# A hybrid RWKV-7 and attention block in fp32 on one core: input norm reordered, POOL's two-tensor work taken out of attention, planner numbers changed

## The chip, the core and the metric

The kernel runs on one core of a Trainium2 chip. The metric is the device time of one execution in microseconds (us); of several executions the median counts. The profile is of one further execution. Its engines are PE (TensorE, matrix products), DVE (VectorE), ACT (ScalarE), POOL (GpSimd) and SP (SyncE, which here issues DMAs). "PEclk" is the clock that PE was granted, as a share of 2.4 GHz; it has two levels, 1.00 and 0.50 (1.2 GHz).

## The reference

```
h     = rms_norm(x, norm_g)                       # x: 512 tokens x 2048 channels
proj  = h @ w_in                                  # 11008 columns = 86 strips of 128
xr, xk, xv, wdown, adown = split(centred_shift(proj[..., :3328], mu))   # strips 0 to 25
z_r, q, k, v, z_a, gates = split(proj[..., 3328:])                      # strips 26 to 85
o_r   = rwkv7_bidir(xr, xk, xv, wdown, adown, ...) * silu(z_r)   # 16 heads of 64, scan over tokens both ways
o_a   = axial_gqa(q, k, v) * silu(z_a)                           # 16 query heads, 4 key heads of 64
merged = sigmoid(g_r) * (o_r @ w_branch_rwkv) + sigmoid(g_a) * (o_a @ w_branch_attn)
out   = rms_norm(x + merged @ w_out, final_norm_g)

def axial_gqa(q, k, v):            # in blocks of 128 queries
    q, k = rope(rms_norm(q)), rope(rms_norm(k))
    p = softmax(q k^T / 8)
    return p v
```

## The kernel before

**Products.** All large products are made in fp32 precision from three passes of a faster format (fp32r): each operand is split into a high part and the rest (`split`, L263: ACT casts the high part, L264; DVE, or POOL where `load` is told so, subtracts, L265). For each of 16 channel tiles of a strip PE does three matmuls of 128x512 (L291): high by high, low by high, high by low. A quarter of a strip is one DMA of 256 KB on SP's queue (`raw`), one cast `wh`, one subtraction `wl` and 12 matmuls. `hh` and `hl` are the high and low part of the normalised, transposed input.

**Stages.** (1) The norm: four tiles of 128 tokens (`x01`, `x23`) are loaded, squared and summed (ACT, partly DVE at L358), scaled by 1/rms in pieces of 512 columns (L371 on POOL, L373 on DVE), transposed by PE (`turn`, L383) and written as `hh` by ACT (L385) and `hl` by DVE (L386); two strips are multiplied beside it. While x is on its way, PE does `warm` transposes of a constant (L394). (2) The RWKV stage: 8 tiles of two heads each. For a tile `stage_a` squares the keys (`sq`, ACT L502), sums them per head on PE (`pss`, L507), takes the root on POOL and spreads it back over PE (`prb`, L516). `tile_task` builds the chunk matrices (`lr`, L637), transposes the factors `BK` to token-major (`tb`, L706), inverts small blocks on DVE (L680, L681) and walks 8 chunks: `pa` (L754), copy `a0s` on ACT, `pu` (L763), copies, `px2` (L770). `stage_e` normalises a tile's output, transposes it (`pg`, L816) and finishes it on DVE (`gc`, L819, L820). `sq` takes its buffer from a ring of four (`temp`) in which `gc` stands too. (3) Attention: 64 units of 128 queries of a head: scores `sc` (L961, L962), maximum on DVE (L964), exp on ACT (`pr`, L967), scaling on POOL (L970), transposes `pT` (L978), split `ph`, `pl` on ACT and DVE, product with the values `po` (L993). Beside it the 16 strips of the RWKV branch's projection are multiplied (`acc<-oq`, below R); their input `oq` takes the buffer of `hh` when the last input strip is done (`or_task`). The first strips of the attention branch's projection (`acc<-oah`, below A) start there as far as heads are done. (4) The rest of A with the merge (`tgm`, L1067, L1068), the output product (L1101 to L1103) and the final norm.

**Order.** PE's instructions stand in the order of the code up to the end of stage 2. A planner (`Weave`) sets that order with planned times: a task says after how many ns it wants to go on (`yield cost, wait, flag`), and in between PE gets "dense" matmuls of the strips (`Dense`), planned at 227 ns each. From stage 3 on a scheduler sets PE's order as well, as it does for the other engines everywhere, by planned times of its own. Each engine then works strictly in its order. `OPT` holds the numbers: `c1` is the planned wait between `pa` and `pu`, `warm` the count of warm-up transposes, `every=2` gives every second `wl` of the R strips and of the input strips left in stage 3 to POOL.

Of the kernel before, what the change touches and what calls it, by code (L numbers as in the profile page):

```python
# [213 lines left out]
OPT = dict(manual=True, tls=True, sub="dve", subwait=47000, fwait=6000, gn=22000, u1=0, u2=0, c1=700, c2=700, c3=1400, fly=3, scale='pool', prb=4, low=1300, warm=24, rwt='tile', every=2, auto=1, man=1)  # L214
# [10 lines left out]
def emit_all(nc, tc, A, out, dbg):  # L225
    ve, ac, po, pe, sp = nc.vector, nc.scalar, nc.gpsimd, nc.tensor, nc.sync

    def f(ap):
# [100 lines left out]
    with tc.tile_pool(name="xps", bufs=5, space=PSUM) as xps:  # L329
# [17 lines left out]
        po.memset(mhalf, -0.5)  # L347
        for tt in range(4):
            sq = rw.tile([128, D], F32, name="xsq", tag="bko")
            ss = rw.tile([128, 6], F32, name="ss", bufs=4)  # L350
            cut = {0: (D, D), 1: (1024, 1024), 2: (D, D), 3: (1024, 1536)}[tt]
            ac.activation(sq[:, 0:cut[0]], xt[tt][:, 0:cut[0]], AF.Square, accum_out=ss[:, 0:1])
            n = 1
            if cut[1] > cut[0]:
                ac.activation(sq[:, cut[0]:cut[1]], xt[tt][:, cut[0]:cut[1]], AF.Square, accum_out=ss[:, 1:2])
                n = 2
            if cut[1] < D:
                ve.scalar_tensor_tensor(out=sq[:, cut[1]:D], in0=xt[tt][:, cut[1]:D], scalar=1.0, in1=xt[tt][:, cut[1]:D],  # L358
                                        op0=ALU.mult, op1=ALU.mult, accum_out=ss[:, n:n + 1])
                n += 1  # L360
# [7 lines left out]
            for c in range(4):
                piece = xt[tt][:, c * 512:(c + 1) * 512]
                if tt == 2 or (tt == 3 and c == 3):  # L370
                    po.tensor_scalar(out=piece, in0=piece, scalar1=ss[:, 5:6], scalar2=0.0, op0=ALU.mult, op1=ALU.add)  # L371
                else:
                    ve.tensor_scalar(out=piece, in0=piece, scalar1=ss[:, 5:6], scalar2=None, op0=ALU.mult)  # L373
        ac.copy(blk, con[:, K_BLK:K_BLK + 128])
        ve.tensor_tensor(out=c0, in0=par[:, P_MU0:P_MU0 + 26], in1=par[:, P_MU1:P_MU1 + 26], op=ALU.add)
        ve.tensor_scalar(out=c0, in0=c0, scalar1=-1.0, scalar2=1.0, op0=ALU.mult, op1=ALU.add)
        ve.tensor_scalar(out=oka, in0=par[:, P_KA:P_KA + 8], scalar1=-1.0, scalar2=1.0, op0=ALU.mult, op1=ALU.add)
        ve.tensor_scalar(out=wah, in0=par[:, P_W0:P_W0 + 32], scalar1=0.5, scalar2=None, op0=ALU.mult)
# [110 lines left out]
    def stage_a(i):  # L489
# [121 lines left out]
    def tile_task(i):  # L611
# [90 lines left out]
        for d in range(2):  # L702
            for g in range(2):
# [334 lines left out]
    def share_r(d):  # L1038
# [132 lines left out]
```

## Time and profile before

| | |
|---|---|
| median of 3 runs | 1744.57 us (1742.69 to 1744.64) |
| the profiled execution | 1745.22 us |
| its span, first to last instruction | 1743.5 us |
| mean granted clock of PE | 0.99 |
| PE / DVE / ACT / POOL busy | 97% / 70% / 49% / 23% of the span |
| stage 1, norm | 0 to about 42 us |
| stage 2, RWKV tiles | to about 1190 us |
| stage 3, attention | to about 1473 us |
| stage 4, A strips, output product, final norm | to the end |

Everything that the span holds beyond PE's busy time is PE's waiting or the ends of the program. So the profile is read from PE's waits: how long, where in the stages, and what ended each. The second thing to read is the granted clock, since a matmul takes about twice as long at 0.50.

### The profile page before, as it was taken

How to read it: one execution, taken by the hardware profiler on the slowest of the kernel's cores; microseconds unless marked ns; L12 is line 12 of the kernel's file. 1: busy time of each engine (PE TensorE's matmuls, PEld its weight loads, DVE VectorE, ACT ScalarE, POOL GpSimd, SP SyncE). 2: the span in 40 equal slices, each digit the busy share in tenths (PEclk: the TensorE clock that was granted, in tenths of full speed). 3: DMA queues.
4: the chain of work that ended last, by engine and by line, in shares of the span. 5: the costliest groups of instructions: out<-in, count | busy, mean ns of one | idle time of the engine just before them, and what ended most of it. 6: DMA issues, size and time to landing. Idle time of an engine off the chain costs nothing. (4 is left out here: it accounts for less than half of the span.)

```text
span 1743.5 us, 26135 instructions
## 1 busy us (share of the span) xinstructions
PE 1694.3 (97%) x8972; PEld 1423.0 (82%) x8972; DVE 1212.0 (70%) x2437; ACT 849.1 (49%) x1955; POOL 393.4 (23%) x523
## 2 busy tenths in 40 slices
PE   7999999999999999999999999999999998999997
PEld 6888888888888887888887888888788887888876
DVE  6577779779689789689679679435888876443352
ACT  6555455455455454454454454544575655322241
POOL 2001031031131121121121121113555543331110
PEclk8999999999999999999999999999999998999999
DMA  6573323323323333333333324235343331444462
GB/s 218 167 230 105 108 60 116 104 80 104 101 85 104 92 91 91 91 98 100 94 93 93 94 67 121 86 103 169 97 133 108 99 97 61 136 130 134 127 181 103
DMA packets 96852, 194.89 MB, mean 112 GB/s; under 512 B 11088, under 2 KB 11344, under 8 KB 95312
## 3 DMA queue, kind: packets, MB, share of 16 engines
q1 hardware_dynamic: 77616, 152.18, 30.1%
q10 hardware_dynamic: 15264, 28.46, 4.5%
q0 software_dynamic: 3840, 12.59, 2.5%
q8 instruction: 72, 1.18, 0.3%
q14 instruction: 60, 0.49, 0.1%
HBM read 162.77 MB, written 30.41 MB: 111 GB/s over the span
## 5 line engine op out<-in xcount | busy, mean ns | idle before, releaser
L291 PE MATMUL acc<-hh,wl 128*128 128x512 f32 (+1 forms) x1388 | 551.6, 397 | 4.0 <-DVE wl L265 4.0
L291 PE MATMUL acc<-hl,wh 128*128 128x512 f32 (+1 forms) x1388 | 551.1, 397 | 2.4 <-DVE hl L386 2.1
L291 PE MATMUL acc<-hh,wh 128*128 128x512 f32 (+1 forms) x1388 | 552.5, 398 | 0.0
L264 ACT CAST wh<-raw 128x512 fp32r<-128x512 f32 x472 | 291.3, 619 | 428.4 <-PE acc L291 286.0
L265 DVE TENSOR_TENSOR wl<-raw,wh 128x512 fp32r<-128x512 f32 x442 | 316.4, 718 | 240.2 <-ACT wh L264 216.6
L291 PEld LDWEIGHTS acc<-hh,wl 128*128 128x128 f32 x1388 | 263.1, 190 | 55.0 <-DVE wl L265 6.1
L291 PEld LDWEIGHTS acc<-hl,wh 128*128 128x128 f32 x1388 | 263.1, 190 | 52.9 <-DVE hl L386 3.5
L291 PEld LDWEIGHTS acc<-hh,wh 128*128 128x128 f32 x1388 | 263.4, 190 | 49.6 <-ACT wh L264 0.3
L741 POOL TENSOR_SCALAR SV<-VT 64x128 f32<-64x128 f32 x256 | 137.4, 537 | 622.7 <-DVE SV L776 262.6
L776 DVE SCALAR_TENSOR_TENSOR SV<-SV,PC,px 64x64 f32<-64x64 f32 x224 | 62.7, 280 | 66.1 <-PE px L770 53.9
L681 DVE TENSOR_TENSOR B<-B,tm 128x30 f32<-128x30 f32 (+14 forms) x240 | 79.1, 330 | 5.4
L291 PE MATMUL acc<-oq,wh 128*128 128x512 f32 x256 | 82.7, 394 | 0.0
L680 DVE TENSOR_TENSOR tm<-B 128x30 f32<-128x30 f32 (+14 forms) x240 | 79.2, 330 | 5.0
L1102 PE MATMUL of<-wl,mh 128*128 128x512 f32 x192 | 74.9, 390 | 1.2 <-DVE wl L265 1.2
L1103 PE MATMUL of<-wh,ml 128*128 128x512 f32 x192 | 74.7, 389 | 0.0
L770 PEld LDWEIGHTS px<-SV,L 128*128 128x128 f32 x512 | 67.0, 191 | 6.9 <-ACT SV L764 1.5
L754 PEld LDWEIGHTS pa<-SV,AL 128*128 128x128 f32 x512 | 66.7, 191 | 4.8
L1101 PE MATMUL of<-wh,mh 128*128 128x512 f32 x192 | 66.1, 389 | 0.0
L754 PE MATMUL pa<-SV,AL 128*128 128x64 f32 x512 | 64.9, 269 | 0.0
L770 PE MATMUL px<-SV,L 128*128 128x64 f32 x512 | 64.7, 269 | 0.0
L291 PE MATMUL acc<-oah,wh 128*128 128x512 f32 x128 | 52.1, 409 | 5.5 <-ACT oah L264 3.4
L778 ACT COPY O<-px 64x128 f32<-64x128 f32 x64 | 16.7, 260 | 81.5 <-DVE SV L776 74.4
(686 smaller groups left out, 2744.1 us busy)
## 6 DMA issues: line engine op xcount, KB each, us to landing
raw<-in_w_in_dram SPq DMA_DIRECT2D x344, 256.0 KB, 3.2
raw<-in_wo_dram SPq DMA_DIRECT2D x64, 256.0 KB, 2.8
fsp<-tg ACTq DMA_DIRECT2D x60, 256.0 KB, 3.0
tsp<-la ACTq DMA_DIRECT2D x32, 256.0 KB, 3.8
la<-tsp SPq DMA_DIRECT2D x8, 1024.0 KB, 5.2
raw<-in_wbr_dram SPq DMA_DIRECT2D x32, 256.0 KB, 2.8
tgm<-fsp POOLq DMA_DIRECT2D x32, 256.0 KB, 3.5
raw<-in_wba_dram SPq DMA_DIRECT2D x32, 256.0 KB, 2.9
```

The lines of the kernel that those rows point to most:

```text
L264: ac.copy(dst_hi, src)
L265: (eng or ve).tensor_tensor(out=dst_lo, in0=src, in1=f(dst_hi), op=ALU.subtract)
L291: pe.matmul(acc[:, tok], lhsT=w[1 if u == 2 else 0][:, j, :], rhs=(xl if u == 1 else xh)[:, kt, tok], start=(kt == 0 and u == 0 and tok.st ...
L680: se.tensor_tensor(out=tv, in0=B[:, 0:s, s:s + 1].to_broadcast([128, s, n]), in1=B[:, s:s + 1, s + 1:32].to_broadcast([128, s, n]), op=ALU ...
L681: se.tensor_tensor(out=B[:, 0:s, s + 1:32], in0=B[:, 0:s, s + 1:32], in1=tv, op=ALU.add)
L741: mv = po.tensor_scalar(out=new[v0:v0 + 64, d, eo], in0=src.unsqueeze(1).to_broadcast([64, 2, C]), scalar1=1.0, scalar2=0.0, op0=ALU.mult, ...
L754: pe.matmul(pa[:, d, eo, :], lhsT=AL[:, d, cc[d], eo, :], rhs=SV[:, d, eo, 0, :], start=True, stop=True)
L770: pe.matmul(px2[:, d, eo, :], lhsT=L2[:, d, cc[d], eo, :], rhs=SV[:, d, eo, 1, :], start=True, stop=True)
L776: mn = ve.scalar_tensor_tensor(out=SN[h, d, eo, 0, :], in0=SV[h, d, eo, 0, :], scalar=PC[h, d, cc[d]:cc[d] + 1], in1=px2[h, d, eo, :], op0 ...
L1101: pe.matmul(acc, lhsT=mh[:, dt, tok(tt)], rhs=w[0], start=(dt == 0), stop=False)
L1102: pe.matmul(acc, lhsT=mh[:, dt, tok(tt)], rhs=w[1], start=False, stop=False)
L1103: pe.matmul(acc, lhsT=ml[:, dt, tok(tt)], rhs=w[0], start=False, stop=(dt == NKT - 1))
```

## The change

It touches five places.

- **Norm.** DVE's half of the squares of token tile 1 is written ahead of the scaling of tile 0; the scaling pieces of tiles 0 and 1 alternate by column (DVE); those of tiles 2 and 3 are written one by one at every fourth `turn` instead of ahead of all. The first `wl` goes to DVE instead of POOL. The small constants `c0`, `oka`, `wah` move behind the third `hl`. `warm` is 34 instead of 24.
- **RWKV tiles.** `c1` is 950 instead of 700. The wait ahead of `pss` is 7000 instead of 1500 (6000 for tile 0). The 16 `tb` transposes are visited twice by 8 instead of four times by 4.
- **Attention.** `every` is 0, so all `wl` are DVE's. `rotate` and the product of the heads' output with its gate move from POOL to DVE. The scaling of `pr` stays on POOL.
- **R strips.** Strips 14 and 15 may be planned only when unit 59 is through (flag `U59`).

```diff
-OPT = dict(..., c1=700, ..., warm=24, rwt='tile', every=2, auto=1, man=1)
+OPT = dict(..., c1=950, ..., warm=34, rwt='tile', every=0, auto=1, man=1)
...
-            first[i]["w"][q] = load(first[i], q, i == 0 and q == 0)
+            first[i]["w"][q] = load(first[i], q)
...
+        def normed(tt, c, by, eng):
+            piece = xt[tt][:, c * 512:(c + 1) * 512]
+            if eng is po:
+                po.tensor_scalar(out=piece, in0=piece, scalar1=by, scalar2=0.0, op0=ALU.mult, op1=ALU.add)
+            else:
+                ve.tensor_scalar(out=piece, in0=piece, scalar1=by, scalar2=None, op0=ALU.mult)
...
+            if tt == 1:
+                with tc.issue_after(half_.ins):
+                    for c in range(4):
+                        for t_ in range(2):
+                            normed(t_, c, inv_rms[t_], ve)
...
         for step in range(NKT):
-            turn(step, 0)
+            low_ = turn(step, 0)
             if 3 <= step < 15:
                 three(0, step - 3, slice(0, 256))
...
+            if step % 4 == 3:
+                normed(2, step // 4, inv_rms[2], po)
+                with tc.issue_after(low_.ins):
+                    normed(3, step // 4, inv_rms[3], ve if step < 12 else po)
...
-        yield 0, 1500 if i else 6000, None
+        yield 0, 7000, None
         pss = g_tile("pss")
...
                 ac.copy(L2b[:, d, 4 * g:4 * g + 4, 0:4:3, :], tb)
-                yield 428, 700, None
+                if g:
+                    yield 856, 1400, None
...
-        po.tensor_tensor(out=sw, in0=sw, in1=rope[:, 1], op=ALU.mult)
+        ve.tensor_tensor(out=sw, in0=sw, in1=rope[:, 1], op=ALU.mult)
...
-                po.tensor_tensor(out=oa, in0=oa, in1=sz, op=ALU.mult)
+                ve.tensor_tensor(out=oa, in0=oa, in1=sz, op=ALU.mult)
...
-        dense.add(dict(src=A["wbr"][d], ..., pre=gate(d, S_GR, wp, "tg", 2)), "or")
+        dense.add(dict(src=A["wbr"][d], ..., pre=gate(d, S_GR, wp, "tg", 2)), "or" if d < 14 else "U59")
```

What the built program makes of it, at three places. DVE at the start, before and then changed (`x01` holds token tiles 0 and 1; `ss` are their sums and roots; L353 is the scaling in the changed code):

```order
L366 TENSOR_SCALAR ss_118<-ss_118 128x1
L373 TENSOR_SCALAR x01_88<-x01_88,ss_118 128x512 x4
L358 SCALAR_TENSOR_TENSOR xsq_126,ss_127<-x01_88 128x1024
L362 TENSOR_REDUCE ss_127<-ss_127 128x1
L366 TENSOR_SCALAR ss_127<-ss_127 128x1
L373 TENSOR_SCALAR x01_88<-x01_88,ss_127 128x512 x4
```

```order
L376 TENSOR_SCALAR ss_118<-ss_118 128x1
L370 SCALAR_TENSOR_TENSOR xsq_122,ss_123<-x01_88 128x1024
L353 TENSOR_SCALAR x01_88<-x01_88,ss_118 128x512 x4
L374 TENSOR_REDUCE ss_123<-ss_123 128x1
L265 TENSOR_TENSOR wl_97<-raw_94,wh_96 128x512
L376 TENSOR_SCALAR ss_123<-ss_123 128x1
L353 TENSOR_SCALAR x01_88<-x01_88,ss_123 128x512 x4
```

Tile 1's squares now come before tile 0's scaling, and a `wl` has come in between.

DVE in the sixth RWKV tile, between the last `gc` of the tile before and the first instruction that reads `pss`, before and then changed (`tm` and `B` are the block inversion):

```order
L820 SCALAR_TENSOR_TENSOR gc_6699<-gc_6699,par_72,sz_6700 128x512
L265 TENSOR_TENSOR wl_6747<-raw_6744,wh_6746 128x512
L681 TENSOR_TENSOR B_6465<-B_6465,tm_6471 128x13x18
L680 TENSOR_TENSOR tm_6471<-B_6465 128x238
L681 TENSOR_TENSOR B_6465<-B_6465,tm_6471 128x14x17
L509 TENSOR_SCALAR rs_6759<-pss_6754 128x8
```

```order
L838 SCALAR_TENSOR_TENSOR gc_6743<-gc_6743,par_72,sz_6744 128x512
L698 TENSOR_TENSOR B_6508<-B_6508,tm_6514 128x13x18
L265 TENSOR_TENSOR wl_6787<-raw_6784,wh_6786 128x512
L697 TENSOR_TENSOR tm_6514<-B_6508 128x238
L698 TENSOR_TENSOR B_6508<-B_6508,tm_6514 128x14x17
L697 TENSOR_TENSOR tm_6514<-B_6508 128x240
L698 TENSOR_TENSOR B_6508<-B_6508,tm_6514 128x15x16
L697 TENSOR_TENSOR tm_6514<-B_6508 128x240
L265 TENSOR_TENSOR wl_6809<-raw_6806,wh_6808 128x512
```

The reader of `pss` stood five rows behind `gc`; now it stands 29 rows behind it, and five `wl` lie in between. On PE this `pss` stands 71 strip matmuls behind the `pg` ahead of it instead of 16. (The first two tiles have no `pg` ahead; for the other six the counts were 47, 22, 45, 16, 43 and 14 and are 68, 33, 54, 71, 36 and 57.)

PE in attention, from the last input strip (`acc<-hh`) to the first R matmul (`acc<-oq`), before and then changed:

```order
L291 MATMUL acc_12377<-hh_79,wl_12400 128x512
L993 MATMUL po_12278<-ph_12236,VS_11359 128x256 x4
L978 MATMUL pT_12389<-con_71,pr_12246 128x128 x4
L993 MATMUL po_12278<-pl_12237,VS_11359 128x256 x4
L978 MATMUL pT_12443<-con_71,pr_12300 128x128 x4
L961 MATMUL sc_12452<-KH_11357,Q_12208 128x512
L962 MATMUL sc_12452<-KL_11358,Q_12208 128x512
L961 MATMUL sc_12477<-KH_11357,Q_12208 128x512
L962 MATMUL sc_12477<-KL_11358,Q_12208 128x512
L993 MATMUL po_12491<-ph_12313,VS_11359 128x256 x4
L978 MATMUL pT_12470<-con_71,pr_12323 128x128 x4
L993 MATMUL po_12491<-pl_12314,VS_11359 128x256 x4
```

```order
L291 MATMUL acc_12261<-hh_79,wl_12327 128x512
L996 MATMUL pT_12230<-con_71,pr_12135 128x128 x4
L1011 MATMUL po_12206<-ph_12168,VS_11442 128x256 x4
L979 MATMUL sc_12239<-KH_11440,Q_11725 128x512
L980 MATMUL sc_12239<-KL_11441,Q_11725 128x512
L1011 MATMUL po_12206<-pl_12169,VS_11442 128x256 x4
L979 MATMUL sc_12276<-KH_11440,Q_11728 128x512
L980 MATMUL sc_12276<-KL_11441,Q_11728 128x512
L291 MATMUL acc_13020<-oq_12445,wh_13002 128x512
L291 MATMUL acc_13159<-oq_12445,wh_13016 128x512
```

Between the two kinds of strip stand 28 attention matmuls before and 16 in the change. Further on, the built order of PE has the 384 R matmuls done ahead of the 61st pair of score matmuls before, and ahead of the 50th in the change: strips 14 and 15 stand behind unit 44, not behind unit 59. The 42 A matmuls that lie inside attention stand behind the 60th pair before and behind the 49th in the change. 48 input-strip matmuls (one strip) that stood behind the first score matmul now stand ahead of it.

## Rows read from the trace of the kernel before

**Rows 1.** Page, part 1: engine, busy us, share of the span, instructions.

```profile
PE 1694.3 (97%) x8972; PEld 1423.0 (82%) x8972; DVE 1212.0 (70%) x2437; ACT 849.1 (49%) x1955; POOL 393.4 (23%) x523
```

**Rows 2.** Waits of PE: engine, tile, line, releaser: total us, times, longest us.

```profile
PE pss L507 <- ACT sq L502: 6.9, 3, 3.1
PE pu L763 <- ACT a0s L757: 6.2, 14, 1.1
```

**Rows 3.** Stretches: length, busy of PE, PEld, DVE, ACT, POOL, PEclk, DMA share, GB/s.

```profile
10.72:14.10 3.38, 0.55 (x5) 0.31 (x3) 3.25 (x6) 0.30 (x2) 1.50 (x1) 1.00 0.99 405
14.13:20.90 6.77, 5.25 (x23) 4.82 (x24) 5.93 (x17) 6.74 (x15) 4.60 (x6) 0.50 0.85 307
671.60:674.90 3.30, 3.30 (x17) 2.71 (x16) 3.23 (x11) 1.71 (x4) 1.65 (x1) 1.00 0.57 202
690.00:693.30 3.30, 3.30 (x9) 2.62 (x8) 2.98 (x8) 0.62 (x1) 1.17 (x1) 0.50 0.28 109
1260.00:1473.00 213.00, 206.12 (x1153) 175.82 (x1151) 165.99 (x346) 131.11 (x267) 103.87 (x116) 1.00 0.31 96
1449.60:1469.60 20.00, 19.29 (x114) 16.40 (x112) 13.26 (x28) 10.92 (x22) 4.76 (x6) 1.00 0.13 41
1471.70:1481.80 10.10, 6.72 (x15) 4.80 (x16) 5.04 (x7) 3.09 (x5) 5.19 (x7) 0.50 0.39 130
```

**Rows 4.** Timeline, start: start us, us, instruction, count [idle before, releaser].

```profile
6.08 5.08 PE L394 MATMUL warm<-con 128*128 128x128 f32 x24 [6.08 <-DMA con<-in_con_dram]
9.99 2.68 DVE L373 TENSOR_SCALAR x<-x,ss 128x512 f32<-128x512 f32 x4 [0.74 <-POOL ss L261]
12.60 1.21 DVE L358 SCALAR_TENSOR_TENSOR xsq<-x 128x1024 f32<-128x1024 f32 x1
14.94 1.67 DVE L373 TENSOR_SCALAR x<-x,ss 128x512 f32<-128x512 f32 x4 [0.67 <-POOL ss L261]
15.48 1.76 PE L383 MATMUL xT<-con,x 128*128 128x128 f32 x7 [4.21 <-DVE x L373]
24.16 0.43 PE L291 MATMUL acc<-hl,wh 128*128 128x256 f32 x1 [1.81 <-DVE hl L386]
```

**Rows 5.** Timeline, RWKV stage: the longest but one wait of `pss`.

```profile
686.52 0.74 DVE L820 SCALAR_TENSOR_TENSOR gc<-gc,par,sz 128x512 f32<-128x512 f32 x1
687.30 0.72 ACT L502 ACTIVATE sq<-k,par 128x512 f32<-128x512 f32 x1 [2.53 <-DVE gc L820]
688.08 1.05 PE L507 MATMUL pss<-con,sq 128*128 128x2 f32 x8 [2.83 <-ACT sq L502]
```

**Rows 6.** Timeline, attention: DVE beside POOL, and PE behind it.

```profile
1236.51 1.70 POOL L265 TENSOR_TENSOR wl<-raw,wh 128x512 fp32r<-128x512 f32 x1 [2.61 <-ACT wh L264]
1237.01 1.75 DVE L265 TENSOR_TENSOR wl<-raw,wh 128x512 fp32r<-128x512 f32 x1
1238.81 0.50 PE L291 MATMUL acc<-hh,wl 128*128 128x512 f32 x1 [3.55 <-DVE wl L265]
...
1306.46 0.98 POOL L970 TENSOR_SCALAR pr<-pr,st__12520 128x512 f32<-128x512 f32 x1 [0.79 <-DVE st__12520 L968]
1306.87 1.11 DVE L1026 TENSOR_TENSOR oq<-oq 128x512 fp32r<-128x512 f32 x1
```

**Rows 7.** DVE by line, 1260 to 1473 us: count | busy, mean ns | idle before.

```profile
L265 DVE TENSOR_TENSOR pl<-pT,ph 128x512 fp32r<-128x512 f32 x60 | 40.6, 684 | 10.9 <-ACT ph L264 10.8
```

**Rows 8.** Timeline, switch from the input strips to the R strips.

```profile
1291.94 0.63 POOL L1022 DMA_DIRECT2D oq<-osp  x1 [1.14 <-PE acc L291]
...
1296.82 0.40 PE L291 MATMUL acc<-oq,wh 128*128 128x512 f32 x1
```

**Rows 9.** PE by line, 1449.6 to 1469.6 us: an A product's pass.

```profile
L291 PE MATMUL acc<-oal,wh 128*128 128x512 f32 x13 | 5.2, 403 | 0.0
```

**Rows 10.** Timeline, end of attention.

```profile
1471.04 1.26 POOL L1001 TENSOR_TENSOR oa<-oa,re 128x512 f32<-128x512 f32 x1 [5.80 <-DVE oa L998]
1473.00 1.22 PE L291 MATMUL acc<-oah,wh 128*128 128x512 f32 x2 [3.44 <-ACT oah L264]
```

More of the change, by code (lines that the diff above doesn't have):

```diff
@@ L211, in step @@
         return True
-OPT = dict(manual=True, tls=True, sub="dve", subwait=47000, fwait=6000, gn=22000, u1=0, u2=0, c1=700, c2=700, c3=1400, fly=3, scale='pool', prb=4, low=1300, warm=24, rwt='tile', every=2, auto=1, man=1)
+OPT = dict(manual=True, tls=True, sub="dve", subwait=47000, fwait=6000, gn=22000, u1=0, u2=0, c1=950, c2=700, c3=1400, fly=3, scale='pool', prb=4, low=1300, warm=34, rwt='tile', every=0, auto=1, man=1)
 def context(nc):
@@ L350, in emit_all @@
             ss = rw.tile([128, 6], F32, name="ss", bufs=4)
[L351 to L360, printed above, removed]
@@ L361, in emit_all @@
-            if n > 1:
-                ve.tensor_reduce(out=ss[:, 3:4], in_=ss[:, 0:n], axis=AX.X, op=ALU.add)
+            cut = 1024 if tt == 1 else 1536 if tt == 3 else D
+            parts = []
+            if cut < D:
+                parts.append((ve, cut, D))
+            parts.append((ac, 0, min(cut, 1024) if tt == 3 else cut))
+            if tt == 3:
+                parts.append((ac, 1024, cut))
+            for n, (eng, c0_, c1_) in enumerate(parts):
+                if eng is ac:
+                    ac.activation(sq[:, c0_:c1_], xt[tt][:, c0_:c1_], AF.Square, accum_out=ss[:, n:n + 1])
+                else:
+                    half_ = ve.scalar_tensor_tensor(out=sq[:, c0_:c1_], in0=xt[tt][:, c0_:c1_], scalar=1.0, in1=xt[tt][:, c0_:c1_],
+                                            op0=ALU.mult, op1=ALU.mult, accum_out=ss[:, n:n + 1])
@@ L363, in emit_all @@
+            tot = ss[:, 0:1]
+            if len(parts) > 1:
+                ve.tensor_reduce(out=ss[:, 3:4], in_=ss[:, 0:len(parts)], axis=AX.X, op=ALU.add)
                 tot = ss[:, 3:4]
-            else:
-                tot = ss[:, 0:1]
             ve.tensor_scalar(out=ss[:, 4:5], in0=tot, scalar1=1.0 / D, scalar2=NORM_EPS, op0=ALU.mult, op1=ALU.add)
             rsqrt(ss[:, 5:6], ss[:, 4:5], 1)
[L368 to L378, printed above, removed]
+            inv_rms.append(ss[:, 5:6])
@@ L385, in turn @@
             ac.activation(hh[:, kt, tok], pt, AF.Copy, scale=pc(P_NG + kt))
-            ve.scalar_tensor_tensor(out=hl[:, kt, tok], in0=pt, scalar=pc(P_NG + kt), in1=f(hh[:, kt, tok]), op0=ALU.mult, op1=ALU.subtract)
+            return ve.scalar_tensor_tensor(out=hl[:, kt, tok], in0=pt, scalar=pc(P_NG + kt), in1=f(hh[:, kt, tok]), op0=ALU.mult, op1=ALU.subtract)
         def three(i, kt, tok=slice(0, T)):
@@ L395, in emit_all @@
         for step in range(NKT):
-            turn(step, 0)
+            low_ = turn(step, 0)
             if 3 <= step < 15:
                 three(0, step - 3, slice(0, 256))
+            if step == 2:
+                ac.copy(blk, con[:, K_BLK:K_BLK + 128])
+                with tc.issue_after(low_.ins):
+                    ve.tensor_tensor(out=c0, in0=par[:, P_MU0:P_MU0 + 26], in1=par[:, P_MU1:P_MU1 + 26], op=ALU.add)
+                    ve.tensor_scalar(out=c0, in0=c0, scalar1=-1.0, scalar2=1.0, op0=ALU.mult, op1=ALU.add)
+                    ve.tensor_scalar(out=oka, in0=par[:, P_KA:P_KA + 8], scalar1=-1.0, scalar2=1.0, op0=ALU.mult, op1=ALU.add)
+                    ve.tensor_scalar(out=wah, in0=par[:, P_W0:P_W0 + 32], scalar1=0.5, scalar2=None, op0=ALU.mult)
+            if step % 4 == 3:
+                normed(2, step // 4, inv_rms[2], po)
+                with tc.issue_after(low_.ins):
+                    normed(3, step // 4, inv_rms[3], ve if step < 12 else po)
         for step in range(NKT + 12):
@@ L1042, in done @@
             ve.scalar_tensor_tensor(out=sr["o"][:, d], in0=gates[S_GR, d], scalar=1.0, in1=acc, op0=ALU.add, op1=ALU.mult)
-        dense.add(dict(src=A["wbr"][d], nq=2, x=lambda: sr["x"], done=done, pre=gate(d, S_GR, wp, "tg", 2)), "or")
+        dense.add(dict(src=A["wbr"][d], nq=2, x=lambda: sr["x"], done=done, pre=gate(d, S_GR, wp, "tg", 2)), "or" if d < 14 else "U59")
     for d in range(NKT):
```

1 line of the change is left out of this document (added).

## The prediction

> **What bounds the kernel now.** I read part 1 of the page first: PE is busy 1694.3 of 1743.5 us, DVE 1212.0 [rows 1]. So the kernel is bound by PE, and only two things can change its time: PE's waits, 49 us with both ends of the program, and the stretches in which PE runs at a granted clock of 0.50. The number of matmuls is all but unchanged. Second, PE's waits by what ended them: the two that one line repeats are `pss` behind `sq`, 6.9 us in 3, and `pu` behind `a0s`, 6.2 us in 14 [rows 2]. Third, the stretches with their clock: right after a long wait PE runs at 0.50 [rows 3]. Two RWKV stretches of 3.30 us show the price: 17 matmul records at 1.00, 9 at 0.50. A stretch at 0.50 thus loses 3.3 x (1 - 9/17) = 1.6 us, and a long wait costs itself and about 1.6 more. Last, the timeline around each place that the change touches [rows 4, 5, 6, 8, 10]. The sum stands against the profiled execution, 1745.2 us, which is 0.65 above the median; the difference is smaller than anything below.
>
> **The change, part by part.**
>
> *Norm: -4.2.* Before, DVE scales tile 0 in four pieces (9.99, 2.68 us, beside POOL), then squares its half of tile 1 (1.21), waits for the root, scales tile 1 (1.67), and PE's second transpose starts at 15.48 after 4.21 us of waiting [rows 4]. Now the squares come first, in part of the time in which DVE waited for tile 0's root, and the pieces of tile 0 have no POOL beside them: 2.68 becomes about 1.67, as tile 1's four took. One `wl` (0.68 [rows 7]) is put in. The path to 15.48 shortens by 1.21 + 1.01 - 0.68 = 1.5; I take 1.4. It could be nothing, because tile 1 must have landed, and the DMA share is 0.99 there [rows 3]. The wait at 24.16 for `hl` (1.81 [rows 4]) stands behind the scaling pieces of tiles 2 and 3 on DVE, which are now spread out: -1.3, and with it the half-clock stretch after it, -1.5 (worked out as above, less a little since DVE nearly bounds there). Range -6.0 to -1.4. The ten more warm transposes fill a time in which PE waits anyway. They are 10 x 5.08/24 = 2.1 us [rows 4], inside the 4.21 us.
>
> The clock is 1.00 from 10.7 us and 0.50 from 14.13 to 20.90, after the long wait [rows 3]. I count nothing for this stretch: ACT is busy 6.74 of its 6.77 us, so a faster PE would wait for ACT.
>
> *The wait ahead of `pss`: -10.1.* `sq` takes its buffer from a ring in which `gc` stands, so it starts only when the last `gc` of the tile before ends: `gc` from 686.52, `sq` from 687.30, `pss` at 688.08 after 2.83 us [rows 5]. PE has nothing to do since the order of its work is fixed. The built order now puts 33 to 71 strip matmuls between `pg` and `pss`; the three that waited had 22, 16 and 14. A strip matmul takes 3.30/17 = 0.19 us [rows 3], so 33 are 6.4 us against 16 x 0.19 + 2.83 = 5.9 needed. The waits go (6.9), and two of the three had a half-clock stretch behind them (2 x 1.6). Range -10.5 to -9.2; at -9.2 the tightest (33) still waits 0.9. What is late next: the rest of `stage_a` and the first chunks of the next tile, by some 5 us. They are planned again behind it; that is in the term for the re-planned order.
>
> *`c1`: -2.8.* 14 waits of `pu` for `a0s`, 6.2 us, the longest 1.1 [rows 2]. 250 ns more of planned distance is one strip matmul more, 0.2 us, under each: 14 x 0.2 = 2.8. Range -5.0 (the delays in ACT fall elsewhere) to 0 (each tile's chunk chain becomes longer and its end late).
>
> *`tb` in two visits: 0.* The transposes, copies and dense matmuls are the same; only the points of re-entry are fewer. I take 0; -1.4 to +0.7, by four waits fewer or more of the mean 6.2/14 us per tile and half of them.
>
> *Start of attention: -5.2.* POOL's `wl` (1.70) and DVE's (1.75) run beside each other at 1236.5, and PE waits 3.55 for DVE's [rows 6]; alone such a subtraction takes 0.68 [rows 7]. With all `wl` on DVE, POOL's share costs DVE 0.68 and both end earlier: 0.68 x 2 against 1.75 from a later start. The wait and its half-clock stretch go, 3.55 + 1.6. Least -1.7: the wait halves, and the clock falls still.
>
> *Rest of attention: +1.5.* 47 instructions move from POOL to DVE (counted in the built order: 29 `wl`, 10 of `rotate`, 8 products of `oa`). At 0.68 [rows 7] they are 32 us more of DVE, less what contention is spared. From 1260 to 1473 DVE is busy 166.0 of 213.0 us and PE 206.1 [rows 3]; with some 24 us more DVE has 190 and still isn't the bound on the mean. In detail:
> the switch from input to R strips +1.8. The R strips' input is asked for at 1291.94, and the first product runs at 1296.82 [rows 8]; 4.9 us were covered by 28 attention matmuls and by the DMAs' early start. 16 are left, at about 0.16 us each 2.6 us, so 2.3 are bare, less something for what is issued earlier. Range 0 to +4 (with a half-clock stretch).
> The end, in which no A strips lie beside the last 14 units, +1.5. In the 20 us from 1449.6 PE has 114 records [rows 3], 38 of them A products (13, 13 and 12 of three passes, one of them shown [rows 9]), at 0.227 us 8.6 us. The other 76 fill 11.4 us; DVE is busy 13.3 there [rows 3], some 10 without what it does for the strips, so PE and DVE run about level and wait for each other now and then. Range 0 to +8.
> POOL's product 1.26 before the last head [rows 10] becomes one of 0.68 on DVE: -0.6. Waits of `pT` for scalings that POOL had behind its two-tensor work: -1.2 (0 to -1.9).
>
> Beside POOL's scaling of `pr`, which stays, a DVE product of `oq` takes 1.11 [rows 6]. The Trainium skill (SBUF — State Buffer, Who interferes with whom) says that a DVE instruction with two inputs in SBUF and a GpSimd instruction that reads SBUF exclude each other fully. This speaks against the change as far as it goes: the work moved to DVE is of just that kind, and the scalings remain. The row shows 0.43 more and not the 0.98 of the whole scaling. By the rule 29 `wl` at 0.98 would be 28 us, an estimate, and the sum 1753 if PE waited for all of it; by the row they are rival A.
>
> *The re-planned order elsewhere: +1.0.* All places of strips against RWKV tiles shift. PE's small waits there are unknown: -2 to +4 by the small waits of today, 6.2 us in 14 [rows 2].
>
> Sum: -4.2 - 10.1 - 2.8 + 0 - 5.2 + 1.5 + 1.0 = -19.8, so 1725.4 against 1745.2.
>
> **The rivals.** *A, DVE gives it back in attention.* The 29 `wl` meet POOL's 64 scalings and each costs 1.11 - 0.68 = 0.43 more, 12.5 us of DVE that PE waits for. Against it: DVE has 47 us free in the 213, some 23 after the move. For it: DVE's work there is bunched by units. Time 1725.4 + 12.5 = 1738, with part of it 1733.
> *B, the end of attention has cover.* The two strips are held for it by their flag. If the scheduler's order meant what the flag says, the wait of 3.44 at 1473 [rows 10] and its stretch at 0.50 (15 records in 10.1 us [rows 3], some 4 us) would go: 1725.4 - 7.4 - 1.5 = 1716.5. Against it: the built order has both strips behind unit 44.
> *C, nothing changes.* The waits go where they were and come back behind the next late step of a tile, since the chain from `gc` to the next tile is no shorter: -13 become 0, attention gives the rest back. 1742 to 1748, in the middle 1745. Against it: 5 us of strip matmuls lie between, and the chunk walk has such work under all of its waits but 14.
> *D, the end runs at half the clock: slower.* The last 14 units hold some 210 matmul records without strips among them, about 210 x 20/114 = 37 us by the mean of that row [rows 3], 32 with their shorter kind. If DVE makes PE wait there so that the clock stays at 0.50, these 32 us double: 1725.4 + 32 = 1757. It decides from 20 us lost on. For it: after the wait at 1473 the clock stays at 0.50 for ten us [rows 3]. Against it: DVE's load and PE's are about level there.
>
> **How the numbers follow.** What a measurement can tell from no change is about 0.2%, 3.5 us. My forecast (1719 to 1731) has 0.60, A 0.15 (1731 to 1741), B 0.13 (1712 to 1719), C 0.05, D 0.07. Range: the forecast, B's upper half and A's lower two thirds, 1716 to 1737, leaves out some 0.2. Faster: forecast, A and B and a bit of C, 0.89; the same 0.05; slower 0.06.
>
> **What would show it.** Norm: the second transpose before 14.5 us, no wait of `hl` over 0.5. `pss`: no wait over 0.5, and no 0.50 between 42 and 1190 us. `c1`: the waits of `pu` under 4 us. Attention: no wait for `wl` near its start; a wait of about 2 us for `oq`; DVE under 90% busy. The end: waits of `sc`, `pT` and `po` for ACT and DVE of 1 to 3 us in sum, at a clock of 1.00. The forecast is wrong if the clock is 0.50 in the last 14 units, or if waits of `wl` appear beside `pr`'s scalings.

## The result, and the profile after

The changed kernel takes 1726.07 us in the median (1724.94 to 1727.28), before 1744.57; the ratio is 0.9899, 95% interval 0.9886 to 0.9912. The forecast was 1725.4, in a range of 1716 to 1737. The span of the profiled execution is 1725.5 us, against 1743.5.

Part 1 of the page after, against [rows 1], and PE's waits after, against [rows 2]:

```profile
PE 1689.8 (98%) x8982; PEld 1421.3 (82%) x8982; DVE 1212.9 (70%) x2485; ACT 849.1 (49%) x1955; POOL 329.9 (19%) x475
```

```profile
PE warm L400 <- DMA con<-in_con_dram: 6.1, 1, 6.1
PE acc L291 <- ACT oah L264: 2.8, 1, 2.8
PE pu L781 <- ACT a0s L775: 2.4, 5, 0.9
PE acc L291 <- DVE tgm L1085: 2.3, 1, 2.3
PE of L1120 <- DVE wl L265: 2.0, 3, 0.7
PE acc L291 <- ACT hh L391: 1.9, 1, 1.9
PE xT L389 <- DVE x L353: 1.6, 1, 1.6
PE acc L291 <- DVE wl L265: 1.5, 2, 1.0
PE acc L291 <- ACT oq L1043: 1.2, 1, 1.2
...
PE pT L996 <- POOL pr L988: 0.6, 1, 0.6
```

`pss` no longer waits at all, `pu` waits 2.4 us instead of 6.2. DVE has 48 instructions more than before and is busy only 0.9 us longer, which was not expected; POOL is busy 63.5 us less.

The start, PE and then DVE, against [rows 4] (start us, us, instruction, count, in brackets the idle time before it and what ended it):

```profile
6.12 5.59 PE L400 MATMUL warm<-con 128*128 128x128 f32 x34 [6.12 <-DMA con<-in_con_dram]
...
13.38 0.98 PE L389 MATMUL xT<-con,x 128*128 128x128 f32 x7 [1.56 <-DVE x L353]
16.32 0.54 PE L291 MATMUL acc<-hh,wh 128*128 128x256 f32 x1 [1.95 <-ACT hh L391]
```

```profile
8.62 1.23 DVE L370 SCALAR_TENSOR_TENSOR xsq<-x 128x1024 f32<-128x1024 f32 x1 [0.51 <-DMA x<-in_x_dram]
...
9.78 1.67 DVE L353 TENSOR_SCALAR x<-x,ss 128x512 f32<-128x512 f32 x4
...
11.43 0.68 DVE L265 TENSOR_TENSOR wl<-raw,wh 128x512 fp32r<-128x512 f32 x1
```

Stretches after (length, busy of PE, PEld, DVE, ACT, POOL, PEclk, DMA share, GB/s), against [rows 3]: the norm's, the start of attention, the switch to the R strips, the last units, and what follows the last `po`:

```profile
16.42:19.78 3.36, 3.28 (x14) 2.99 (x15) 3.33 (x14) 3.36 (x10) 3.08 (x4) 0.50 0.94 345
1222.00:1258.00 36.00, 36.00 (x187) 30.46 (x186) 28.43 (x60) 21.23 (x43) 8.16 (x9) 1.00 0.35 110
1265.70:1269.00 3.30, 3.14 (x7) 2.49 (x8) 3.30 (x9) 2.66 (x6) 2.37 (x4) 0.50 1.03 401
1425.00:1450.00 25.00, 22.48 (x137) 17.72 (x138) 21.44 (x54) 18.23 (x40) 9.22 (x12) 1.00 0.00 1
1453.50:1463.60 10.10, 7.79 (x19) 5.34 (x18) 4.83 (x7) 2.72 (x5) 5.29 (x7) 0.50 0.46 146
```

The wait of 3.55 us at the start of attention [rows 6] and the stretch at half the clock behind it are gone (PE is busy 36.00 of 36.00). A new half-clock stretch stands at the switch. The last units run at 1.00, with DVE busy 21.4 of 25.0 us.

### The profile page after: what moved, and what is told of

It reads as the page before. It is cut to its first block, busy times and chain, and to the rows that moved or that the text cites. A ratio compares the mean times of both kernels' runs of the same rounds, so it can differ in the third digit from the quotient of the medians.

```text
span 1725.5 us, 26201 instructions
## 1 busy us (share of the span) xinstructions
PE 1689.8 (98%) x8982; PEld 1421.3 (82%) x8982; DVE 1212.9 (70%) x2485; ACT 849.1 (49%) x1955; POOL 329.9 (19%) x475
## 4 chain that ended last, share of the span: by engine, by line
PE 89%; DVE 4%; ACT 2%; DMA 2%; issue 2%; POOL 0%; ACTq 0%; POOLq 0%; DVEq 0%; SPq 0%
PE acc L291 62%; PE px L788 3%; PE pa L772 3%; PE of L1120 2%; PE of L1121 2%; PE of L1119 2%; PE pu L781 2%; PE lr L654 2%; PE po L1011 2%; PE pT L996 1%; PE pq L731 1%; PE px L744 1%; PE sc L979 1%; DVE wl L265 1%; PE sc L980 1%
## 5 line engine op out<-in xcount | busy, mean ns | idle before, releaser
L265 DVE TENSOR_TENSOR wl<-raw,wh 128x512 fp32r<-128x512 f32 x472 | 333.1, 708 | 256.6 <-ACT wh L264 242.8
L291 PEld LDWEIGHTS acc<-oq,wh 128*128 128x128 f32 x256 | 47.9, 190 | 12.0 <-ACT oq L1043 1.7
```

The lines of the kernel that those rows point to most:

```text
L265: (eng or ve).tensor_tensor(out=dst_lo, in0=src, in1=f(dst_hi), op=ALU.subtract)
L291: pe.matmul(acc[:, tok], lhsT=w[1 if u == 2 else 0][:, j, :], rhs=(xl if u == 1 else xh)[:, kt, tok], start=(kt == 0 and u == 0 and tok.st ...
```

## The experiments

Each run is the kernel before or the changed kernel with one edit, as its expectation says. All ratios are against the kernel before on the same chip, and 0.001 is 1.7 us. (An execution in which a half-clock stretch is longer or shorter differs by some us, which the intervals contain.)

**The wait ahead of `pss` alone.**

```diff
-        yield 0, 1500 if i else 6000, None
+        yield 0, 7000, None
```

> The kernel before with the planned wait ahead of pss alone at 7000 instead of 1500 (6000 for tile 0). My theory: the three waits of pss behind sq (6.9 us) and the two half-clock stretches behind them (1.6 each) go and nothing takes their place: 10.1 us faster, about 1734.5, ratio 0.9942. Rival (C of the prediction): the wait moves to the next step of the tile, and the time is within 2 us of before. A third: the later part of stage_a costs more waits of pu or wl; then 4 to 7 us faster.

Measured: 1734.21 us, ratio 0.9942 (0.9929 to 0.9954), 10.1 us faster, as expected. The trace has no wait of `pss` and no half-clock stretch from 20 to 1228 us. One wait of `prb` of 0.9 us came, and `pu` waits 5.1 us instead of 6.2; the two about cancel. Rival C falls.

**A fifth buffer in the ring that `sq` and `gc` share.** The order on PE stays row for row.

```diff
-        return rw.tile([128, T], dt, name=nm, tag="e", bufs=4)
+        return rw.tile([128, T], dt, name=nm, tag="e", bufs=5)
```

> The kernel before with a fifth buffer in the ring that sq and gc share; the planned numbers and the order on PE stay as before, row for row. My theory says that sq waits for gc's buffer and for nothing else: the three waits of pss (6.9 us) go or fall under 1 us and their half-clock stretches with them, 7 to 10 us faster, about 1735.5, with no strip moved. Rival: what makes sq late is the chain itself (ACT's own queue, or the keys), and only more strips ahead of pss help: the waits stay over 5 us and the time within 2 us of before.

Measured: 1736.64 us, ratio 0.9955 (0.9940 to 0.9970), 7.8 us faster. PE's waits in it:

```profile
PE pu L763 <- ACT a0s L757: 6.2, 14, 1.1
PE acc L291 <- DVE wl L265: 4.1, 2, 3.6
...
PE prb L516 <- DVE rb L512: 3.3, 4, 1.3
```

The three waits of `pss` (6.9 us) are gone with not one matmul moved, so the ring was their cause. What was next late is seen too: `prb`, 20 strip matmuls behind `pss`, waits 3.3 us in 4. Here `pss` runs at 684.24 us, but DVE has the `gc` of the tile before to finish (686.54, 0.75 us) ahead of the first instruction that reads it (687.52). With the planned wait `gc` is done by then.

**`tb` in two visits alone.**

```diff
-                yield 428, 700, None
+                if g:
+                    yield 856, 1400, None
```

> The kernel before with the transposes tb in two visits of 8 alone. My theory: nothing of its own, -1.4 to +0.7 us, about 1744, ratio 1.0000. Rival: the re-planned order decides, since every place behind the first tb shifts; by the c1 run, in which prb and pss got other waits, that is up to 4 us either way, in waits of pss, prb and pu that stand at other tiles than before.

Measured: 1735.97 us, ratio 0.9949 (0.9934 to 0.9964): 8.9 us faster. My theory (nothing) falls, and the rival had the kind right and the size too small. PE's waits:

```profile
PE pu L764 <- ACT a0s L758: 4.5, 10, 0.9
...
PE prb L516 <- DVE rb L512: 3.6, 3, 1.7
...
PE pss L507 <- ACT sq L502: 0.4, 1, 0.4
```

All but 0.4 us of the waits of `pss` is gone here too, though the planned wait is the old one. In the built order `pss` now stands 49, 26, 0, 28, 1 and 30 strip matmuls behind `pg` (before 47, 22, 45, 16, 43, 14): the edit shifts where the planner wakes each task, and no `pss` is left at 14 or 16. At 0 and 1 `sq` has its buffer ahead of the last `gc` of the tile before and runs 7.7 and 7.6 us before `pss`; these two tiles have waits of `prb` instead, 1.64 and 1.73 us. The first of them, on ACT, PE, DVE and PE:

```profile
543.93 0.72 ACT L502 ACTIVATE sq<-k,par 128x512 f32<-128x512 f32 x1 [1.83 <-issue]
...
551.64 0.95 PE L507 MATMUL pss<-con,sq 128*128 128x2 f32 x8
...
557.35 0.75 DVE L821 SCALAR_TENSOR_TENSOR gc<-gc,par,sz 128x512 f32<-128x512 f32 x1
...
558.89 0.63 PE L516 MATMUL prb<-con,rb 128*128 128x128 f32 x4 [1.64 <-DVE rb L512]
```

Not all of the 8.9 us is `pss`: the wait of 3.55 us at the start of attention is 1.44 in this run, with no half-clock stretch behind it.

**The changed kernel with `tb` back in four visits, and with the wait back.**

```diff
-                if g:
-                    yield 856, 1400, None
+                yield 428, 700, None
```

> The changed kernel with tb put back to four visits of 4 alone. The built order has pss 66, 31, 48, 63, 27 and 45 strip matmuls behind pg. If tb's 9 us of the run with tb alone were its own (fewer visits, fewer re-entries), it is 9 us slower, 1735. My theory: they were the waits of pss, which the planned wait takes away by itself; nothing is left to gain: within 2 us of the changed kernel, 1724 to 1728.

Measured: 1725.7 us, ratio 0.9887 (0.9870 to 0.9903). Level with the changed kernel (0.9899): beside the longer wait, `tb` is worth nothing that the comparison can tell.

```diff
-        yield 0, 7000, None
+        yield 0, 1500 if i else 6000, None
```

> The changed kernel with the wait ahead of pss alone put back to 1500 (6000 for tile 0). The built order has pss 41, 7, 27, 44, 9 and 30 strip matmuls behind pg in the six tiles, instead of 68, 33, 54, 71, 36 and 57. If the gains of single edits add up, it is 10 us slower than the changed kernel, 1736. My theory now: tb's two visits alone moved pss to other places and took most of the same waits, so the credit is shared; at 7 and 9 some 1.5 to 3 us of waits of pss or prb are left with their half-clock stretch: 2 to 6 us slower, 1728 to 1732.

Measured: 1739.52 us, ratio 0.9963 (0.9948 to 0.9978), some 11 us slower than the changed kernel. My theory here (2 to 6 us) fell. PE's waits, and one of the two places (first the stretch behind the wait, then the one that holds it):

```profile
PE pss L524 <- ACT sq L519: 8.0, 2, 4.1
```

```profile
428.60:435.20 6.60, 5.71 (x17) 4.85 (x18) 5.42 (x16) 1.34 (x2) 2.37 (x2) 0.50 0.24 79
421.90:428.40 6.50, 3.44 (x20) 2.55 (x18) 6.36 (x15) 2.08 (x5) 0.00 (x0) 1.00 0.29 83
```

There are two waits, at the two tiles with 7 and 9 matmuls ahead. They are 4.1 and 3.8 us long, not 1.5 to 3, and each has a half-clock stretch of 6.8 us behind it: 17 matmul records in 6.60 us, where 3.30 us held 17 at 1.00 [rows 3]. The profiled execution is 12.7 us longer than that of the changed kernel (spans of 1738.2 and 1725.5): 8.0 of waiting and up to 2 x 3.3 of clock, less some 1.6 for the 3.4 us stretch of the norm, which this execution did not have.

**`c1` alone.**

```diff
-OPT = dict(..., c1=700, ...)
+OPT = dict(..., c1=950, ...)
```

> The kernel before with c1 alone at 950 instead of 700. My theory: the 14 waits of pu for a0s (6.2 us) lose 0.2 us each, 2.8 us faster, about 1741.8, ratio 0.9984; the changed kernel's trace has 2.4 us left in 5 waits, by which it would be 3.8. Rival: each chunk is a matmul longer and the end of a tile comes later, so that nothing is gained (within 1 us), or the re-planned order brings the pss waits to other places (up to 5 us either way).

Measured: 1740.7 us, ratio 0.9978 (0.9969 to 0.9987), 3.8 us faster. `pu` waits 1.3 us in 5 instead of 6.2 in 14, so 4.9 less. But the places of all tiles moved with it (`pss` at 39, 2, 21, 36, 0 and 14): `pss` waits 4.5 instead of 6.9, `prb` 3.2 instead of nothing, and the `wl` at the start of attention 1.6 instead of 3.55, without a half-clock stretch. The 3.8 us are a sum of these, not the term's own size.

**The norm alone, and 24 warm transposes in the changed kernel.** The diff of the first is the norm's part of the change with `warm=34`.

```diff
-            first[i]["w"][q] = load(first[i], q, i == 0 and q == 0)
+            first[i]["w"][q] = load(first[i], q)
...
+                            normed(t_, c, inv_rms[t_], ve)
...
+                    normed(3, step // 4, inv_rms[3], ve if step < 12 else po)
```

> The kernel before with the norm's part alone (squares of tile 1 first, alternating pieces, pieces of tiles 2 and 3 between the transposes, first wl on DVE, constants later, 34 warm transposes). My theory: 4.2 us faster, about 1740.4, ratio 0.9976; the last transpose of the norm starts at about 37.5 instead of 41.5 us and all behind it stands in the same distances. Rival: the half-clock stretch is only moved, and the gain is the shorter wait alone, 1.5 to 2.5 us.

Measured: 1742.2 us, ratio 0.9987 (0.9978 to 0.9996): 2.3 us faster, between 0.7 and 3.8. In place the gain is there; the weight loads of the norm's 64 transposes (ns min/median/max, first and last start in us) in this run, in the changed kernel and in the run with `c1` alone, whose norm is that of before:

```profile
L389 PEld LDWEIGHTS xT<-con,x x64: 137/140/225, 11.4 to 37.3; 128*128 128x128 f32 x64
```

```profile
L389 PEld LDWEIGHTS xT<-con,x x64: 137/140/224, 11.4 to 37.5; 128*128 128x128 f32 x64
```

```profile
L383 PEld LDWEIGHTS xT<-con,x x64: 137/141/230, 10.7 to 40.8; 128*128 128x128 f32 x64
```

The last transpose starts at 37.3 to 37.5 instead of 40.8 (41.4 in the profiled execution of before, 39.6 in the run that moves POOL's work, also with the norm of before). At the end of this execution 2.1 us are left of it, because two waits that the edit did not touch, of `pss` and of `wl`, have longer half-clock stretches behind them:

```profile
941.30:948.00 6.70, 6.70 (x19) 5.45 (x19) 5.05 (x14) 0.62 (x1) 1.74 (x1) 0.50 0.26 81
1234.90:1241.60 6.70, 5.32 (x13) 4.16 (x14) 4.76 (x10) 3.25 (x7) 5.19 (x5) 0.50 0.45 144
```

Before, these two stretches were 3.4 us long each. The edit is not needed for the longer ones: with the norm of before, the wait of 3.57 us for `wl` had 3.4 us at half the clock behind it in the run of the wait alone and one of 3.61 had 6.8 with the fifth buffer, and a wait of `pss` of 3.15 had 6.8 with `c1` alone. What sets their length stays open.

```diff
-OPT = dict(..., warm=34, ...)
+OPT = dict(..., warm=24, ...)
```

> The changed kernel with 24 warm transposes instead of 34. My theory: the ten more only fill a wait: within 1 us of the changed kernel, 1726, and the wait ahead of the second tile's transposes is 3.7 instead of 1.56 us. Rival: they keep the clock up: then the half-clock stretch at the start is 6.8 us long instead of 3.4 and the kernel 1 to 3 us slower, 1727 to 1729.

Measured: 1726.76 us, ratio 0.9894 (0.9878 to 0.9911), level with the changed kernel. The wait ahead of tile 1's transposes was 2.2 us, not 3.7, and the half-clock stretch was 6.8 long, as the rival says:

```profile
14.40:21.10 6.70, 4.90 (x23) 4.44 (x21) 5.63 (x18) 6.41 (x16) 5.01 (x7) 0.50 0.78 299
```

The last transpose starts at 38.1 instead of 37.5, and at the end the comparison can tell no difference. ACT is busy 6.41 of the stretch's 6.70 us, much as before [rows 3], so a faster PE would have had little to gain.

**POOL's two-tensor work to DVE alone.**

```diff
-OPT = dict(..., every=2, ...)
+OPT = dict(..., every=0, ...)
...
-        po.tensor_tensor(out=sw, in0=sw, in1=rope[:, 1], op=ALU.mult)
+        ve.tensor_tensor(out=sw, in0=sw, in1=rope[:, 1], op=ALU.mult)
...
-                po.tensor_tensor(out=oa, in0=oa, in1=sz, op=ALU.mult)
+                ve.tensor_tensor(out=oa, in0=oa, in1=sz, op=ALU.mult)
```

> The kernel before with POOL's two-tensor work of attention given to DVE alone (every=0, rotate, the product of oa with its gate). My theory: the wait of 3.55 us for wl at the start of attention goes with its half-clock stretch (-5.2), the rest of attention gives 1.5 back: 3.7 us faster, about 1740.9, ratio 0.9979, and the 47 moved instructions add their 32 us to DVE's busy time less what contention is spared, so 20 to 28 us more. Rival A: the moved subtractions meet POOL's scalings of pr at 1.11 us each; DVE's busy time in attention rises by over 30 us and the kernel is slower by up to 8 us.

Measured: 1739.12 us, ratio 0.9979 (0.9969 to 0.9989), 3.7 us faster: the time came as expected, the load did not. Part 1 of its page:

```profile
PE 1694.2 (98%) x8972; PEld 1423.0 (82%) x8972; DVE 1215.7 (70%) x2484; ACT 851.8 (49%) x1955; POOL 334.6 (19%) x476
```

47 instructions more cost DVE 3.7 us instead of 20 to 28, while POOL lost 58.8 us. At 0.68 each the 47 are 32 us, so DVE's other instructions lost some 28 us, spread over many lines. The subtractions `wl` over the attention stage, before, in this run and in the changed kernel (count | busy, mean ns | idle before):

```profile
L265 DVE TENSOR_TENSOR wl<-raw,wh 128x512 fp32r<-128x512 f32 x30 | 26.8, 892 | 3.4 <-ACT wh L264 3.4
```

```profile
L265 DVE TENSOR_TENSOR wl<-raw,wh 128x512 fp32r<-128x512 f32 x50 | 36.7, 734 | 4.0 <-ACT wh L264 3.3 <-PE pT L978 0.4
```

```profile
L265 DVE TENSOR_TENSOR wl<-raw,wh 128x512 fp32r<-128x512 f32 x45 | 32.9, 734 | 7.3 <-ACT wh L264 7.3
```

`wl` takes 734 instead of 892 ns; 684 is the price alone [rows 7]. `oq`, beside which POOL's scalings stay, is not shorter in this run (892 ns, before 880). The largest single share is that of 64 products with one element per partition (`st`, L965: the row maximum times a factor), before and in this run (length of the stretch, busy of these on DVE, PEclk, DMA share, GB/s):

```profile
1190.00:1480.00 290.00, 17.22 (x64) 0.98 0.34 105
```

```profile
1190.00:1480.00 290.00, 10.00 (x64) 0.98 0.35 106
```

Most of them take 0.16 us. The long ones end together with an instruction of POOL; one of before:

```profile
1399.15 1.29 POOL L1001 TENSOR_TENSOR oa<-oa,re 128x512 f32<-128x512 f32 x1
...
1399.82 1.30 DVE L965 TENSOR_TENSOR st__13357<-st__13357,qs 128x1 f32<-128x1 f32 x1
...
1400.42 0.68 POOL L970 TENSOR_SCALAR pr<-pr,st__13292 128x512 f32<-128x512 f32 x1
```

It ends at 1401.12, POOL's second instruction at 1401.10. In both pairs of [rows 6] DVE's instruction of 128x512 ends 0.54 or 0.55 us behind POOL's (1238.76 and 1238.21, 1307.98 and 1307.44). In these rows a partner on POOL costs DVE what is left of the partner when DVE's instruction starts.

**More cover at the end: strips held back.** Built with and without its flag `U59`, the changed kernel has the same order on DVE, ACT, POOL and SP, and on PE but for one pair of neighbours (`pT` and `po`): the flag sets planned times, and from stage 3 on the scheduler doesn't go by them. (No run takes the flag out of the changed kernel.) Here the last four R strips are tied to units on PE itself, and all but the first nine matmuls of the second A strip wait for the last `po`.

```diff
+        with tc.issue_after(held[spec["hold"]]) if spec.get("hold") and (q, jj) >= spec.get("at", (0, 0)) else nullcontext():
+            pe.matmul(acc[:, tok], ...)
...
+    HOLD = {12: 43, 13: 47, 14: 53, 15: 61}
...
+            dense.add(dict(src=A["wba"][d], ..., hold="po" if d == 1 else None, at=(0, 9)), "or")
```

> The changed kernel with its last four R strips tied on PE behind the scores of units 43, 47, 53 and 61 and 12 matmuls of the second A strip behind the last po. My theory of the end (rival B of the prediction): the wait of 2.77 for the last oah, the 2.31 behind it and the half-clock stretch of 10 us go, and the 2.3 us of small waits in the last 14 units shrink: 5 to 9 us faster than the changed kernel, 1717 to 1721. Rival: taking strips from units 39 to 49 gives these units waits of their own, since DVE and PE run level without strips: 1724 to 1728. If DVE bounds the whole of attention, the end is only moved and the time stays within 2 us.

Measured: 1728.36 us, ratio 0.9905 (0.9890 to 0.9920), no gain: the first rival. PE's waits:

```profile
PE sc L981 <- ACT pr L987: 5.4, 10, 1.0
PE acc L292 <- DVE tgm L1088: 3.5, 1, 3.5
...
PE acc L292 <- ACT oah L264: 0.6, 1, 0.6
```

The wait for `oah` fell from 2.8 to 0.6, as meant. But `sc` waits 5.4 us in 10 (1.2 in 3 after the change) in the units that lost their strips, and the wait for `tgm` grew to 3.5: more cover did not shorten it. POOL's row in the changed kernel's timeline shows what that wait hangs on:

```profile
1454.43 1.69 POOL L1053 DMA_DIRECT2D tgm<-fsp  x3 [7.57 <-PE acc L291]
```

The first A gate is asked for only behind the last head: by the code, its buffer lies in a pool (`br`) that opens where attention's closes.

**That gate early, and 12 matmuls of one A strip behind the last `po`.**

```diff
+        if u == 52:
+            gate(0, S_GA, wp, "tga", 1)()
...
-        t_ = at.tile([128, T], F32, name="re", tag="re", bufs=3)
+        t_ = at.tile([128, T], F32, name="re", tag="re", bufs=2)
...
-            dense.add(dict(src=A["wba"][d], ..., pre=gate(d, S_GA, br, "tgm", 3)), "or")
+            dense.add(dict(src=A["wba"][d], ..., pre=gate(d, S_GA, br, "tgm", 3) if d else lambda: None, late=(0, 9) if d == 1 else (9, 0)), "or")
```

> The changed kernel with the first A gate (tgm of strip 0) loaded at unit 52 into a buffer of its own (the ring re has 2 buffers instead of 3 for the room), and 12 matmuls of the second A strip tied behind the last po. In the changed kernel's trace that gate is asked for only at 1454.4, behind the last po, and PE waits 2.77 for oah and 2.31 for tgm, and runs at half the clock for 10.2 us. My theory: both waits go under 1 us in sum: 4 us, and 3 to 4 more where the clock stays up: 1718 to 1722. Rival: the 12 matmuls are missed by the units from which they are taken, and the wait for tgm goes over to strip 1, whose gate still comes late: 1724 to 1728.

Measured: 1719.87 us, ratio 0.9850 (0.9835 to 0.9865), faster than both kernels. Its PE at the end:

```profile
1451.43 0.73 PE L292 MATMUL acc<-oah,wh 128*128 128x512 f32 x2 [0.56 <-ACT oah L264]
...
1453.67 0.51 PE L292 MATMUL acc<-oah,wh 128*128 128x512 f32 x1 [0.31 <-DVE tgm L1089]
```

```profile
1449.00:1457.00 8.00, 7.13 (x28) 4.86 (x28) 6.33 (x8) 2.36 (x5) 3.04 (x5) 1.00 0.40 141
```

2.8 and 2.3 us of waiting became 0.56 and 0.31, and the clock stays at 1.00. The small waits of the last units are 2.7 us against 2.3, and one of 0.5 for an earlier `oah` came, so the 12 matmuls are hardly missed. The two parts of the edit were not run apart; but in the run before, the matmuls took the wait for `oah` to 0.6 and left that for `tgm`, so the second is the early gate's.

The same with `tb` in four visits:

```diff
-                if g:
-                    yield 856, 1400, None
+                yield 428, 700, None
```

> The kernel of e11_end with tb back in four visits of 4. By the run without tb's two visits, which stood level with the changed kernel (0.9887 against 0.9899), this should stand level with e11_end (0.985): 1717 to 1721. It tells whether the gain at the end of attention (0.5%) holds under another planned order: if it was luck of one order, this run is back at 1724 to 1727.

Measured: 1720.94 us, ratio 0.9858 (0.9841 to 0.9874). The gain at the end holds under another planned order.

## Why the prediction was right, step by step

**`pss`: right.** The waits and their stretches went, 10.1 us alone, with the ring as their cause (the fifth buffer shows it, with PE's order unchanged). What was to be late next appeared as waits of `prb` (0.9 us with the wait alone, none in the changed kernel).

**`tb`: 0 was right only in company.** By itself the edit is worth 8.9 us: its trace has 6.5 us less of `pss`, 2.1 less at the start of attention, both with their stretches, and 3.6 more of `prb`. Beside the longer wait it is worth nothing. The failed step is "the transposes, copies and dense matmuls are the same; only the points of re-entry are fewer": in a planned order a point of re-entry sets where everything behind it lands, and the term for that, -2 to +4, was several times too narrow for the edit alone. (The range of -1.4 to +0.7 does not come out of its row either: four waits of 6.2/14 are 1.8.) The five single edits give 10.1 + 8.9 + 3.8 + 3.7 + 2.3 = 28.8 us, the change about 17.6. The difference is for the most part waits that several edits take: those of `pss` by the wait and by `tb`, that at the start of attention by `tb`, by `c1` and by POOL's work. Undoing showed it for `tb` and the wait; for the others it is read from the traces. The sum of the prediction held because it took each wait once.

**`c1`: -2.8 predicted; `pu`'s waits fell by 3.8** (6.2 to 2.4), while waits of strips for `wl` in the RWKV stage rose by 1.0 (1.02 at 540 us and 0.51 at 671, 0.48 before). That `c1` brought these is not shown.

**Norm: -4.2 predicted; 3.9 earlier in place, 2.3 us (0.7 to 3.8) faster alone.** Three parts were mis-sized, and that they balanced to 3.9 is luck. Tile 1's transposes start 2.1 earlier (15.48 to 13.38), not 1.4; the pieces of tile 0 take the 1.67 that was taken for them. The wait for `hl` went wholly, but 1.95 for `hh` on ACT came. And the 1.5 for the half-clock stretch behind `hl` were a property of the profiled execution: with the same norm the runs of the single edits of the wait, of `c1` and of `tb` had a wait of 1.98 at 24.3 and no such stretch, and their last transposes start at 40.5 to 40.8 instead of 41.4. Against these the norm gains 3.0 to 3.5 in place.

**Attention.** The start gave its 5.2. The switch to the R strips cost 3.2, not 1.8: waits of 0.62, 1.23, 0.16 and 0.47 us where there were 0.9 in sum, and a half-clock stretch of 3.4 us (1.6), inside the range of 0 to 4. The end's small waits are 2.3 us against 0.7, so +1.6 where 1.5 was taken, at a clock of 1.00; rival D falls. Between the two, 1.9 us of waits are gone (1.15 of `pT` for a scaling, the rest of `sc`; 1.2 predicted), and the last `oah` gained 0.7 (0.6). Added up, -5.2 + 3.2 + 1.6 - 1.9 - 0.7 = -3.0 against -3.7.

**DVE's load: wrong, without harm.** The step "with some 24 us more DVE has 190" failed: 47 moved instructions cost 3.7 us. The price was read from instructions that ran alone (0.68), but what had stood beside POOL's instructions on DVE had paid already, the one-element products most of all. Two instructions with two inputs each, one on either engine, took 1.70 and 1.75 [rows 6]; one behind the other on DVE they take 1.37. The Trainium skill (SBUF — State Buffer, Who interferes with whom) says that a DVE instruction with two inputs in SBUF contends with a GpSimd instruction that reads SBUF, and that the port pair which they share is an exclusive lock. The rows agree (one-element products that end 0.02 us behind POOL's instruction). I weighed the sentence on one side only: it spoke for the change as well, since the move took the longest partners away. I also read [rows 6] wrongly as a price below the rule's: the product of `oq` started when 0.57 of the scaling were left and ended 0.54 behind it. Rival A's price, 0.43 for each `wl` beside a scaling, came from one row; over the 45 `wl` of the stage the mean is 0.05 above 0.68, 2.3 us in all. It stems from eight of them that started while a scaling ran and took 0.72 to 1.15 us.

**B and C.** B fell as the built order had said, since the strips were not held. Held in truth they gave nothing either: the units that lost their strips waited 4.2 us more (`sc`, 1.2 to 5.4), and one of the end's two waits had another cause, the late gate. C fell with the run of the wait alone.

**The sum.** By these parts the change gives 10.1 + 2.8 + 3.9 + 3.0 = 19.8 us; the spans of the two profiled executions differ by 18.0, the medians by 18.5. The other 1.3 to 1.8 us are not placed; the prediction had put 1.0 at the order elsewhere.

## What to carry to other kernels

An order that is planned ahead makes single edits poor evidence: an edit that only changes when a task is woken was worth 9 us alone and nothing beside a planned wait of the right length, so undo each edit from the finished version as well. When instructions of two engines lengthen each other, cost a moved one also by what the others no longer lose to it, and not by its duration alone. Before adding cover to a wait, look at when the late operand was asked for.

## What the runs showed of the hardware

- A wait does not have one price in clock. Behind a wait of 3.4 us for `oah` the clock was 0.50 for 10.2 us before [rows 3] [rows 10] and for 3.4 us in the run with the fifth buffer:

```profile
1465.80:1469.00 3.20, 2.93 (x6) 1.78 (x6) 1.39 (x2) 1.23 (x3) 1.67 (x3) 0.50 0.20 56
1469.20:1475.90 6.70, 5.13 (x22) 4.17 (x23) 4.39 (x6) 1.76 (x3) 3.62 (x4) 1.00 0.54 173
```

  Waits of 3.1 to 3.6 us had stretches of 3.4 or 6.8 us; one of 1.81 had 3.4 (before), one of 1.98 none (the run of the wait alone). At some 1.6 us for each 3.3 us at half the clock, a term that is read from one execution can be off by that much, and by 3 us, at a single wait.
- POOL's two-tensor instructions cost DVE nearly what doing the work itself costs: 47 of them moved, POOL -58.8 us, DVE +3.7 us. An instruction of one element per partition took 1.30 us instead of 0.16 because it ended only with POOL's.
